# Encoder block on one core: five branch gates in the entry stage, the residual rows' work at the output projection, operands ahead of those rows in the second phase

## The chip, the cores and the metric

One Trainium2 chip, one of its cores. The metric is the device time of one execution in microseconds (us); the kernel before takes 1377.97 us as the median of three runs (1374.08 to 1382.24). A chip core has TensorE (PE, with PEld for its weight loads), VectorE (DVE), ScalarE (ACT), GpSimd (POOL) and SyncE (SP), each with an instruction stream of its own that is worked off in order; SP, ACT and POOL issue the transfers (DMA).

## The reference, cut to what matters

One encoder layer over 768 tokens of width 1024 (a prompt of 512 and a sample of 256, which are not mixed), in float32:

```python
h = layer_norm(x, ln_in_g, ln_in_b)
proj = h @ w_in + b_in                 # 512 pool | 3072 hyena | 2048 gate columns
a, u3, gl = proj[..., :512], proj[..., 512:3584], proj[..., 3584:]
ya = pool_branch(a, ...)               # four window means minus self, group linear, projection
yb = hyena_branch(u3, ...)             # short conv, two gated long FFT convolutions, projection
g = sigmoid(gl)                        # 2 x 1024 branch gates
m = g[:, :, 0] * ya + g[:, :, 1] * yb
h = layer_norm(DN_ALPHA * h + m @ w_o + b_o, ln1_g, ln1_b)
u = relu(h @ w_ff1 + b_ff1)
h = layer_norm(DN_ALPHA * h + (u * u) @ w_ff2 + b_ff2, ln2_g, ln2_b)
```

## The kernel before, in words

Every product is made of three matmuls, since each float32 operand is split into a high and a low part of a shorter format: ACT copies the raw tile to the high part (`whi`, L98), DVE computes the low part (`wlo`, L90), and PE multiplies high by high, low by high and high by low. `wsplit` (L92) does this for a weight tile that SP loads. So each weight tile costs one DMA on SP, one ACT instruction and one DVE instruction, and PE can't start on it before all three.

The program runs through these stages; the times are where they stand in the trace of before.

- Entry (0 to 45 us): layer norm of x, transposes to `hT_h`, `hT_l` (both parts of h, with the channels on the partitions). The normalised rows without scale are kept in DRAM as `d_h`.
- Entry stage (45 to 375 us): 24 jobs, each one 128-channel tile of the hyena columns (48 matmuls of 128x384 into the PSUM tiles `pa` and `pb`, short convolution, transposes `pta`, `ptb`). Between them run eight `filter_unit`s, which build the long filters' spectra: `pg` matmuls, then DVE and ACT work, a norm (`pn`), the parts `pmh` (ACT) and `pml` (DVE), and the `pk` matmuls. A list `order` with `k_after` sets after which job a filter unit starts; its second half comes after the next job.
- Before the units (375 to 400 us): three `gate_tile`s (16 tiles of 128 gate columns in all; 48 matmuls into a `pp` tile, Sigmoid on ACT, the result to DRAM as `d_s`) and the split of the transform matrix `cu` (L545 to L550).
- Units (400 to 641 us): eight hyena `unit`s, each a chain of transforms (`pf`, `p`, `pi` matmuls, with combining work on DVE between them); between units stand further gate tiles, as many as the tuple in L680 says, and four `pool_in` tiles, which also write `pp`.
- Pool windows (641 to 691 us): the window sums `pw` on DVE, group linear `pq`, the loads and splits of the hyena result `zT_h`, `zT_l`.
- hyena_out and pool_out (691 to 791 us): eight pairs, 48 `pb` and 24 `pa` matmuls each; after each of the first six a `residual_job` (L782 to L797) loads a row tile of `d_h` by POOL, multiplies it by alpha*ln_in_g, adds alpha*ln_in_b + b_o, and writes it back.
- Output projection (791 to 865 us): two groups of three row tiles by eight k steps; the `hr` rows are read from `d_h` and added (L828).
- Second phase (865 us to the end): the MLP in a scheme of seven products per block (`S forms` and the first `EARLY` products ahead, then `up_pair`s, then the down phase with products 0 to 6 and the residual rows `res` loaded by the class `Late`, L1159 to L1169).

The instruction order of each engine is not that of the Python text alone: tiles rotate through a few buffers, and a planner puts each engine's instructions in an order by their dependences. So gate matmuls fall into the chains of the units wherever these leave PE free.

Of the kernel before, what the change touches and what calls it, by code (L numbers as in the profile page):

```python
# [10 lines left out]
F32 = mybir.dt.float32  # L11
# [32 lines left out]
H = T // 2  # L44
EARLY = 7
PLAIN = 7
# [3 lines left out]
def hybrid_encoder(ctx, tc, ins, y_a, y_b):  # L50
# [387 lines left out]
    with ExitStack() as pr_stack:  # L438
# [66 lines left out]
        def x1_job(j):  # L505
            folded_tile(j, d_x1, j)

        order = [(v_job, j) for j in range(8)]
        for c in range(4):
# [3 lines left out]
        for i, (job, j) in enumerate(order):  # L513
            job(j)
            for it in pending:
                for _ in it:
                    pass
            pending = []
            if i in k_after:
                n = k_after[i]  # L520
                it = filter_unit(n % 2, n // 2)
                next(it)
                pending.append(it)
    ew_stack.close()
    k_stack.close()
# [4 lines left out]
    with ExitStack() as t_stack:  # L530
# [8 lines left out]

        gates = list(range(16))  # L540
        for _ in range(3):
            gate_tile(gates.pop(0))
# [135 lines left out]
        for n in range(8):  # L678
            unit(n // 2, n % 2)
            for _ in range((1, 1, 2, 1, 2, 0, 1, 2)[n]):  # L680
                gate_tile(gates.pop(0))
# [76 lines left out]
    def hyena_out(j):  # L758
        w = wsplit(ins["w_hy"][j])
        pb = pst("pp", "pb")  # L760
        proj(pb, w, 8, zT_h, zT_l)
        s = zl.tile([P, T], F32, tag="gt1", name="gt1", bufs=2)
        nc.sync.dma_start(s, d_s[8 + j])
        dve.tensor_tensor(by_halves(s), by_halves(pb), by_halves(s), op=ALU.mult)
        return s

    def pool_out(j, g1t):
        w = wsplit(ins["w_pp"][j], 512)
        pa = pst("pk", "pa")
        proj(pa, w, 4, ph_h, ph_l)  # L770
        s = zl.tile([P, T], F32, tag="gt0", name="gt0", bufs=2)
        nc.sync.dma_start(s, d_s[j])
        dve.tensor_tensor(by_halves(s), by_halves(pa), by_halves(s), op=ALU.mult)
        dve.tensor_tensor(s, s, g1t, op=ALU.add)
        act.copy(mT_h[:, j, :], s)
        lo_of(mT_l[:, j, :], s, mT_h[:, j, :])

    wp_stack.close()
    rj = r_stack.enter_context(pool_of("rj", 1, "right"))
    rows = {}  # L780

    def residual_job(tt):  # L782

        if not rows:
            ag, ab = (row_bc(rj, n) for n in ("ln_in_g", "ln_in_b"))
            bo = rj.tile([P, D], F32, tag="rr", name="bo_bc", bufs=2)
            nc.sync.dma_start(bo, ins["b_o"].partition_broadcast(P))
            act.activation(ag, ag, AF.Copy, scale=ALPHA)
            act.activation(ab, ab, AF.Copy, scale=ALPHA)
            dve.tensor_tensor(ab, ab, bo, op=ALU.add)  # L790
            rows["r"] = (ag, ab)
        ag, ab = rows["r"]
        t = rj.tile([P, D], F32, tag="rr", name="hres", bufs=2)
        pool.dma_start(t, d_h[tt])
        dve.tensor_tensor(t, t, ag, op=ALU.mult)
        dve.tensor_tensor(t, t, ab, op=ALU.add)
        pool.dma_start(d_h[tt], t)  # L797

    prev = hyena_out(0)
    for j in range(8):  # L800
        nxt = hyena_out(j + 1) if j < 7 else None
        pool_out(j, prev)
        prev = nxt
        if j < 6:
            residual_job(j)
    r_stack.close()
# [15 lines left out]
    raw1 = ep.tile([P, 8, H], F32, name="raw1")  # L822
    g1, b1 = (row_bc(ep, n) for n in ("ln1_g", "ln1_b"))

    def add_acc(dst, accs, halves=(0, 1)):
# [26 lines left out]
    for gr in range(2):  # L852
        accs = [[pst("acc", f"ac{t}{c}") for c in range(2)] for t in range(3)]
        hrs = []
        for t in range(3):
            hr = ep.tile([P, D], F32, tag="hr1", name="hr1", bufs=3)
            nc.sync.dma_start(hr, d_h[gr * 3 + t])
            hrs.append(hr)
        for k in range(8):
# [150 lines left out]

    ahead = {1: 7, 3: 8, 4: 9, 6: 10, 7: 11, 9: 12, 10: 13, 12: 14, 13: 15}
    first_us, first_ws = [], []
# [91 lines left out]
    def down_chunk(units, started=None):  # L1104
# [14 lines left out]

        def product(i, wsrc, out, dst, op, first):  # L1120
            us, ws = [], []
            for g in units:
                us.append(u_form(g, i))
                ws.append(split2(wsrc(g), 512, "w"))
            for t in range(3):
                o = out[t] if out else pst("y", "y")
                mult(o, us, ws, t, first)
                evacuate(dst[0], t, dst[1], o, op)

        add, sub = ALU.add, ALU.subtract  # L1130
        if started:
            for t in range(3):
                evacuate(0, t, 0, x[t])
        else:
            product(0, lambda g: b[g](0, 0), x, (0, 0), add, True)
        product(1, lambda g: b[g](1, 0), None, (0, 0), add, True)
        product(3, lambda g: grow(g, b[g](0, 0), b[g](0, 1)), z, (1, 1), add, True)
        product(4, lambda g: grow(g, run[g], b[g](1, 1)), x, (0, 1), sub, False)
# [20 lines left out]
    class Late:  # L1159


        def __init__(self):
            self.t = None

        def __getitem__(self, key):
            if self.t is None:
                self.t = rs_.tile([P, 6, D], F32, name="res")
                for tt in range(6):
                    nc.sync.dma_start(self.t[:, tt, :], d_h[tt])  # L1169
            return self.t[key]  # L1170
# [143 lines left out]
```

## Time and profile before

| | kernel before |
|---|---|
| median of three runs | 1377.97 us (1374.08 to 1382.24) |
| profiled execution | 1377.59 us, span 1375.8 us |
| PE busy | 1292.1 us, 94% of the span |
| DVE busy | 1053.1 us, 77% |
| ACT busy | 636.1 us, 46% |
| POOL busy | 92.2 us, 7% |
| mean granted clock of PE | 0.98 |
| HBM read and written | 162.79 and 68.03 MB, 168 GB/s |

The profiled execution lies 0.4 us under the median. The span is measured from the first to the last instruction; 1.8 us of the execution lie around it. Of the span PE was idle for 83.7 us (1375.8 less 1292.1), of which about 16 lie before the first matmul and 10 after the last. The granted clock is the share of its full rate that TensorE was given; it has two levels, 2.4 GHz (1.00) and 1.2 GHz (0.50), so a window's mean between them tells how much of it was spent at the lower one.

### The profile page before, as it was taken

How to read it: one execution, taken by the hardware profiler on the slowest of the kernel's cores; microseconds unless marked ns; L12 is line 12 of the kernel's file. 1: busy time of each engine (PE TensorE's matmuls, PEld its weight loads, DVE VectorE, ACT ScalarE, POOL GpSimd, SP SyncE). 2: the span in 40 equal slices, each digit the busy share in tenths (PEclk: the TensorE clock that was granted, in tenths of full speed). 3: DMA queues.
4: the chain of work that ended last, by engine and by line, in shares of the span. 5: the costliest groups of instructions: out<-in, count | busy, mean ns of one | idle time of the engine just before them, and what ended most of it. 6: DMA issues, size and time to landing. Idle time of an engine off the chain costs nothing. (4 is left out here: it accounts for less than half of the span.)

```text
span 1375.8 us, 19326 instructions
## 1 busy us (share of the span) xinstructions
PE 1292.1 (94%) x7314; PEld 1190.1 (87%) x7314; DVE 1053.1 (77%) x1625; ACT 636.1 (46%) x1026; POOL 92.2 (7%) x166
## 2 busy tenths in 40 slices
PE   5989999799989999999998999989999997999997
PEld 3879988799989999999998977879999986888885
DVE  7788888789547786878865447988877847997778
ACT  6967767566442232223421234545555643444340
POOL 1000000000000110102010000001211100000000
PEclk9999999899999999999999999999999999999999
DMA  7223442342373544434666365477756559854312
GB/s 284 85 88 119 127 138 91 113 134 101 124 273 100 189 138 162 161 120 158 198 203 214 113 228 199 140 250 283 274 186 210 190 183 313 302 179 133 93 59 92
DMA packets 94998, 232.08 MB, mean 169 GB/s; under 512 B 9936, under 2 KB 34072, under 8 KB 94905
## 3 DMA queue, kind: packets, MB, share of 16 engines
q1 hardware_dynamic: 59504, 162.50, 35.6%
q0 software_dynamic: 12896, 45.62, 8.9%
q10 hardware_dynamic: 22504, 22.73, 5.0%
q8 instruction: 57, 0.93, 0.3%
q14 instruction: 37, 0.30, 0.1%
HBM read 162.79 MB, written 68.03 MB: 168 GB/s over the span
## 5 line engine op out<-in xcount | busy, mean ns | idle before, releaser
L90 DVE TENSOR_TENSOR wlo<-raw,whi 128x1024 fp32r<-128x1024 f32 (+1 forms) x94 | 110.2, 1172 | 60.0 <-ACT whi L98 42.7
L98 ACT CAST whi<-raw 128x1024 fp32r<-128x1024 f32 (+1 forms) x76 | 76.2, 1007 | 140.5 <-PE pp L122 46.3
L1075 ACT CAST uhi<-ur 128x768 fp32r<-128x768 f32 x51 | 42.5, 835 | 111.6 <-PE x L1048 44.0
L1048 PE MATMUL x<-wlo,uhi 128*128 128x512 f32 x180 | 70.4, 392 | 0.0
L1049 PE MATMUL x<-whi,ulo 128*128 128x512 f32 x180 | 69.9, 389 | 0.0
L1047 PE MATMUL x<-whi,uhi 128*128 128x512 f32 x180 | 69.6, 389 | 0.0
L90 DVE TENSOR_TENSOR ulo<-ur,uhi 128x768 fp32r<-128x768 f32 x51 | 48.6, 953 | 15.9 <-ACT uhi L1075 15.8
L111 PE MATMUL pa<-hT_h,whi 128*128 128x384 f32 x176 | 60.3, 343 | 0.5 <-ACT whi L98 0.5
L111 PE MATMUL pa<-hT_h,wlo 128*128 128x384 f32 x176 | 60.5, 344 | 0.0
L111 PE MATMUL pa<-hT_l,whi 128*128 128x384 f32 x176 | 60.2, 342 | 0.0
L111 PE MATMUL pb<-hT_h,wlo 128*128 128x384 f32 x176 | 60.0, 341 | 0.0
L111 PE MATMUL pb<-hT_l,whi 128*128 128x384 f32 x176 | 59.9, 341 | 0.0
L111 PE MATMUL pb<-hT_h,whi 128*128 128x384 f32 x176 | 59.9, 340 | 0.0
L111 PE MATMUL pk<-pmh,ck_h 128*128 128x256 f32 x160 | 45.8, 303 | 13.4 <-ACT pmh L393 13.4
L569 ACT CAST vh<-t 128x512 fp32r<-128x512 f32 x24 | 14.9, 621 | 88.5 <-DVE t L568 88.5
L121 PE MATMUL pp<-hT_h,whi 128*128 128x384 f32 x160 | 54.0, 338 | 0.0
L122 PE MATMUL pp<-hT_l,whi 128*128 128x384 f32 x160 | 54.0, 338 | 0.0
L120 PE MATMUL pp<-hT_l,whi 128*128 128x384 f32 x160 | 54.0, 337 | 0.0
L123 PE MATMUL pp<-hT_h,wlo 128*128 128x384 f32 x160 | 53.9, 337 | 0.0
L124 PE MATMUL pp<-hT_h,wlo 128*128 128x384 f32 x160 | 53.8, 336 | 0.0
L119 PE MATMUL pp<-hT_h,whi 128*128 128x384 f32 x160 | 53.8, 336 | 0.0
L111 PE MATMUL pk<-pml,ck_h 128*128 128x256 f32 x160 | 47.8, 303 | 1.8 <-DVE pml L90 1.8
(341 smaller groups left out, 4440.6 us busy)
## 6 DMA issues: line engine op xcount, KB each, us to landing
raw<-in_w_in SPq DMA_DIRECT2D x44, 512.0 KB, 3.7
ur<-d_u SPq DMA_DIRECT2D x51, 384.0 KB, 3.1
raw<-in_w_ff SPq DMA_DIRECT2D x32, 512.0 KB, 3.9
w<-in_w_ff SPq DMA_DIRECT2D x64, 256.0 KB, 5.3
d_k<-ko POOLq DMA_DIRECT2D x24, 512.0 KB, 3.1
kt<-d_k SPq DMA_DIRECT2D x24, 512.0 KB, 3.5
d_u<-us POOLq DMA_DIRECT2D x56, 192.0 KB, 4.3
d_u<-u ACTq DMA_DIRECT2D x50, 192.0 KB, 3.3
```

The lines of the kernel that those rows point to most:

```text
L90: (eng or dve).tensor_tensor(dst, src, hi.bitcast(F32), op=ALU.subtract)
L98: act.copy(hi[:, :n], raw[:, :n])
L111: pe.matmul(out, l, r, start=(n == 0), stop=(n == len(seq) - 1))
L119: pe.matmul(a, wh[:, ws], xh[:, k, :H], start=first, stop=False)
L120: pe.matmul(a, wh[:, ws], xl[:, k, :H], start=False, stop=False)
L121: pe.matmul(b, wh[:, ws], xh[:, k, H:T], start=first, stop=False)
L122: pe.matmul(b, wh[:, ws], xl[:, k, H:T], start=False, stop=False)
L123: pe.matmul(a, wl[:, ws], xh[:, k, :H], start=False, stop=last)
L124: pe.matmul(b, wl[:, ws], xh[:, k, H:T], start=False, stop=last)
L1047: pe.matmul(out, a, h, start=first and j == 0, stop=False, skip_group_check=not first)
L1048: pe.matmul(out, a, m, start=False, stop=False, skip_group_check=not first)
L1049: pe.matmul(out, l, h, start=False, stop=j == n - 1, skip_group_check=not first)
```

## The change

Four edits stand in one diff.

1. Five of the sixteen branch gates (columns 0 to 4 of the pool branch's gate) are computed in the entry stage by a new `early_gate`, after the first half of a filter unit, in `pa` and `pb`. They are stored before the sigmoid (ACT Identity), and `pool_out` applies the Sigmoid in place after loading such a gate. Ahead of the units stand four gate tiles instead of three, and the tuple of gate tiles between the units falls from (1, 1, 2, 1, 2, 0, 1, 2) to (1, 1, 1, 0, 1, 0, 0, 1), so that two remain behind them instead of three.
2. `residual_job` is gone. The rows alpha*ln_in_g and alpha*ln_in_b + b_o are loaded at the output projection (three broadcasts of 512 KB by SP), and each `hr` row tile gets its multiplication and addition there.
3. `EARLY` is 8 instead of 7, and the table `ahead` follows.
4. At the start of the down phase the operands of products 1 and 3 are loaded and split before the started product's sums are evacuated, and `Late` loads a half row when it is first asked for, instead of six whole row tiles at the first access.

```diff
-EARLY = 7
+EARLY = 8
...
+        def early_gate(j):
+
+            w = wsplit(ins["w_in"][G_T + j])
+            ps = (pst("pa", "pa"), pst("pb", "pb"))
+            st = sg.tile([P, T], F32, tag="st", name="st")
+            for dst, sl in zip(ps, (slice(0, H), slice(H, T))):
+                acc(dst[:, :H], [(w[0][:, k * P : (k + 1) * P], w[1][:, k * P : (k + 1) * P], hT_h[:, k, sl], hT_l[:, k, sl])
+                                 for k in range(8)])
+                act.activation(st[:, sl], dst[:, :H], AF.Identity, bias=col("b_in", G_T + j), scale=1.0)
+            act.dma_start(d_s[j], st)
+            plain_gates.add(j)
...
                 pending.append(it)
+                if i in (2, 6, 8, 10, 12):
+                    early_gate(gates.pop(0))
...
-        for _ in range(3):
+        for _ in range(4):
             gate_tile(gates.pop(0))
...
-            for _ in range((1, 1, 2, 1, 2, 0, 1, 2)[n]):
+            for _ in range((1, 1, 1, 0, 1, 0, 0, 1)[n]):
                 gate_tile(gates.pop(0))
...
         nc.sync.dma_start(s, d_s[j])
+        if j in plain_gates:
+            act.activation(s, s, AF.Sigmoid)
         dve.tensor_tensor(by_halves(s), by_halves(pa), by_halves(s), op=ALU.mult)
...
-        t = rj.tile([P, D], F32, tag="rr", name="hres", bufs=2)
-        pool.dma_start(t, d_h[tt])
-        dve.tensor_tensor(t, t, ag, op=ALU.mult)
-        dve.tensor_tensor(t, t, ab, op=ALU.add)
-        pool.dma_start(d_h[tt], t)
...
+    for dst, name in ((ar[:, 0], "ln_in_g"), (ar[:, 1], "ln_in_b"), (bo, "b_o")):
+        nc.sync.dma_start(dst, ins[name].partition_broadcast(P))
+    act.activation(ar[:, 0], ar[:, 0], AF.Copy, scale=ALPHA)
+    dve.scalar_tensor_tensor(ar[:, 1], ar[:, 1], ALPHA, bo, op0=ALU.mult, op1=ALU.add)
...
             nc.sync.dma_start(hr, d_h[gr * 3 + t])
+            dve.tensor_tensor(hr, hr, ar[:, 0], op=ALU.mult)
+            dve.tensor_tensor(hr, hr, ar[:, 1], op=ALU.add)
...
-    ahead = {1: 7, 3: 8, 4: 9, 6: 10, 7: 11, 9: 12, 10: 13, 12: 14, 13: 15}
+    ahead = {1: 8, 3: 9, 5: 10, 6: 11, 8: 12, 10: 13, 11: 14, 13: 15}
...
         if started:
+            one = operands(1, lambda g: b[g](1, 0))
+            three = operands(3, t1)
             for t in range(3):
                 evacuate(0, t, 0, x[t])
+            multiply(one, None, (0, 0), add, True)
+            multiply(three, z, (1, 1), add, True)
...
-                for tt in range(6):
-                    nc.sync.dma_start(self.t[:, tt, :], d_h[tt])
+            tt, cs = key[1], key[2]
+            for c in range(2):
+                if (tt, c) not in self.got and cs.start in (None, c * 512):
+                    self.got.add((tt, c))
+                    sl = slice(c * 512, (c + 1) * 512)
+                    nc.sync.dma_start(self.t[:, tt, sl], d_h[tt][:, sl])
```

On PE in the entry stage, the matmuls between the norm `pn` of the first filter unit and the first `pk` matmul of its spectrum were none; before:

```order
287 L111 MATMUL pb<-hT_h,whi 128x384
288 L111 MATMUL pb<-hT_l,whi 128x384
289 L422 MATMUL pn<-ident,nr 128x1 x2
290 L111 MATMUL pk<-pmh,ck_h 128x256 x2
291 L485 MATMUL pta<-ident,ft 128x128 x4
292 L489 MATMUL ptb<-ident,ft 128x128 x2
293 L111 MATMUL pa<-hT_h,wlo 128x384
```

and after the change, where 18 matmuls of a gate (`pa`, then `pb`) stand between the two:

```order
291 L111 MATMUL pa<-hT_l,whi 128x384
292 L422 MATMUL pn<-ident,nr 128x1 x2
293 L111 MATMUL pa<-hT_h,wlo 128x384
294 L111 MATMUL pa<-hT_h,whi 128x384
295 L111 MATMUL pa<-hT_l,whi 128x384
296 L111 MATMUL pa<-hT_h,wlo 128x384
297 L111 MATMUL pa<-hT_h,whi 128x384
```

For the second unit's first spectrum it is the other way round. Before, 15 `pa` matmuls followed its `pn`:

```order
475 L111 MATMUL pa<-hT_h,wlo 128x384
476 L422 MATMUL pn<-ident,nr 128x1 x2
477 L111 MATMUL pa<-hT_h,whi 128x384
478 L111 MATMUL pa<-hT_l,whi 128x384
479 L111 MATMUL pa<-hT_h,wlo 128x384
480 L111 MATMUL pa<-hT_h,whi 128x384
```

and after the change its `pk` follows at once:

```order
472 L111 MATMUL pb<-hT_l,whi 128x384
473 L422 MATMUL pn<-ident,nr 128x1 x2
474 L111 MATMUL pk<-pmh,ck_h 128x256 x2
475 L485 MATMUL pta<-ident,ft 128x128 x4
476 L489 MATMUL ptb<-ident,ft 128x128 x2
477 L111 MATMUL pk<-pml,ck_h 128x256
```

On PE at the end of the units, the last `p` matmul of the eighth unit was followed by 97 gate matmuls (`pp`); before:

```order
3692 L111 MATMUL p_6301<-cu_h,vh 128x128
3693 L111 MATMUL p_6301<-cu_l,vh 128x128
3694 L111 MATMUL p_6301<-cu_h,vl 128x128
3695 L124 MATMUL pp<-hT_h,wlo 128x384
3696 L119 MATMUL pp<-hT_h,whi 128x384
3697 L120 MATMUL pp<-hT_l,whi 128x384
3698 L121 MATMUL pp<-hT_h,whi 128x384
```

and after the change by the group linear of the pool branch (`pq`); the `pp` matmuls all stand earlier:

```order
3890 L111 MATMUL p_6427<-cu_h,vh 128x128
3891 L111 MATMUL p_6427<-cu_l,vh 128x128
3892 L111 MATMUL p_6427<-cu_h,vl 128x128
3893 L111 MATMUL pq<-qh,wph 128x512
3894 L111 MATMUL pq<-ql,wph 128x512
3895 L111 MATMUL pq<-qh,wpl 128x512
3896 L111 MATMUL pq<-qh,wph 128x256
```

From the last `pi` matmul of the seventh unit to that point there were 111 `pp` matmuls, and there are 16 now; behind it, up to the first `pa` matmul, there were 193 `pp`, 24 `pq` and 64 `pb`, and there are 24 `pq` and 115 `pb`.

On SP at the start of the down phase, the six residual row tiles (`res`) stood behind the operands of product 1 (`ur` and `w`) and ahead of those of product 3; before:

```order
218 L1081 DMA ur<-d_u 128x768
219 L1097 DMA w_11007<-in_w_ff 128x512 x2
220 L1081 DMA ur<-d_u 128x768
221 L1097 DMA w_11008<-in_w_ff 128x512 x2
222 L1169 DMA res<-d_h 128x1024 x6
223 L1081 DMA ur<-d_u 128x768
224 L1097 DMA w_11007<-in_w_ff 128x512 x4
225 L1081 DMA ur<-d_u 128x768
226 L1097 DMA w_11008<-in_w_ff 128x512 x4
```

and after the change the half rows stand behind both:

```order
209 L1088 DMA ur<-d_u 128x768
210 L1104 DMA w_10998<-in_w_ff 128x512 x2
211 L1088 DMA ur<-d_u 128x768
212 L1104 DMA w_10999<-in_w_ff 128x512 x2
213 L1088 DMA ur<-d_u 128x768
214 L1104 DMA w_10998<-in_w_ff 128x512 x4
215 L1088 DMA ur<-d_u 128x768
216 L1104 DMA w_10999<-in_w_ff 128x512 x4
217 L1192 DMA res<-d_h 128x512 x6
```

## Rows read from the trace of the kernel before

**Rows 1.** The head of the page: the span, and the line of TensorE (PE) with busy us, share of the span and number of instructions.

```profile
span 1375.8 us, 19326 instructions
...
PE 1292.1 (94%) x7314; PEld 1190.1 (87%) x7314; DVE 1053.1 (77%) x1625; ACT 636.1 (46%) x1026; POOL 92.2 (7%) x166
```

**Rows 2.** The waits of PE over the whole span; columns: what waited and for what, us in total, times, longest us.

```profile
PE pk L111 <- ACT pmh L393: 13.4, 8, 2.8
PE pb L123 <- DVE wlo L90: 7.8, 2, 5.5
PE z L1047 <- ACT whi L1075: 7.3, 1, 7.3
PE pi L111 <- ACT vh L569: 5.4, 1, 5.4
PE z L912 <- ACT whi L922: 2.8, 1, 2.8
```

**Rows 3.** PE and the others in four stretches of 25 us; columns: from:to, length, busy us with (xcount) of PE, PEld, DVE, ACT, POOL, then the granted clock of PE, the DMA share and GB/s.

```profile
75.00:100.00 25.00, 22.06 (x125) 20.21 (x126) 20.84 (x48) 14.68 (x30) 1.06 (x2) 0.86 0.39 122
250.00:275.00 25.00, 22.26 (x127) 20.31 (x127) 17.84 (x40) 15.29 (x34) 1.07 (x2) 0.88 0.39 121
400.00:425.00 25.00, 19.65 (x132) 19.33 (x132) 14.74 (x18) 6.62 (x11) 0.00 (x0) 0.86 0.54 188
725.00:750.00 25.00, 19.50 (x99) 19.19 (x98) 14.04 (x15) 3.68 (x5) 2.67 (x5) 0.86 0.63 213
```

**Rows 4.** The same view and columns by stage: the entry stage, the last two units' end (from the last `pi` matmul of unit 6 to the last `p` matmul of unit 7), from there to the first `pa` matmul of the pool branch, and the start of the second phase.

```profile
45.00:375.00 330.00, 311.44 (x1910) 290.47 (x1910) 271.73 (x530) 218.48 (x431) 17.39 (x32) 0.96 0.36 117
601.80:641.10 39.30, 39.21 (x269) 37.56 (x268) 31.34 (x42) 12.55 (x22) 3.61 (x4) 1.00 0.24 81
641.10:691.40 50.30, 49.13 (x281) 47.85 (x281) 44.85 (x52) 23.16 (x36) 5.35 (x6) 1.00 0.61 208
1126.90:1146.00 19.10, 9.62 (x39) 6.47 (x37) 10.49 (x13) 5.21 (x6) 0.00 (x0) 0.94 1.00 376
```

**Rows 5.** The same view of the instructions of one tile alone: the first two rows are of `pp` (columns PE, PEld, ACT), the third of `pb` (PE, PEld, DVE, ACT), the fourth of `pq` (PE, PEld, DVE).

```profile
601.80:641.10 39.30, 21.35 (x112) 18.89 (x112) 2.39 (x6) 1.00 0.24 81
641.10:691.40 50.30, 34.02 (x193) 33.16 (x192) 5.09 (x9) 1.00 0.61 208
...
641.10:691.40 50.30, 11.62 (x64) 11.11 (x65) 0.96 (x1) 0.00 (x0) 1.00 0.61 208
...
641.10:691.40 50.30, 5.62 (x24) 4.16 (x24) 4.30 (x4) 1.00 0.61 208
```

**Rows 6.** The timeline of PE; columns: start, us, engine and line, operation, out<-in, then in brackets the idle time before it and what ended it. The first two are the first and the 91st matmul of one unbroken row of gate matmuls, the third is the first `pk` matmul of a filter spectrum in the entry stage.

```profile
641.13 0.34 PE L119 MATMUL pp<-hT_h,whi 128*128 128x384 f32 x1
...
656.73 0.33 PE L119 MATMUL pp<-hT_h,whi 128*128 128x384 f32 x1
...
245.53 0.50 PE L111 MATMUL pk<-pmh,ck_h 128*128 128x256 f32 x2 [2.75 <-ACT pmh L393]
```

**Rows 7.** The timeline around 405 us, of ACT, of DVE and of PE (one of the last `pf` matmuls ahead of a wait).

```profile
404.76 0.62 ACT L549 CAST cu_h<-craw 128x512 fp32r<-128x512 f32 x1 [1.48 <-DMA craw<-in_cu]
...
408.53 1.22 DVE L566 TENSOR_TENSOR t<-pf,kt 128x1024 f32<-128x1024 f32 x1
...
402.93 0.28 PE L111 MATMUL pf<-abh,cu_l 128*128 128x256 f32 x1
```

**Rows 8.** The timeline of DVE at the end of the units: two low halves of gate weights that are computed there.

```profile
605.47 1.22 DVE L90 TENSOR_TENSOR wlo<-raw,whi 128x1024 fp32r<-128x1024 f32 x1
...
622.90 1.22 DVE L90 TENSOR_TENSOR wlo<-raw,whi 128x1024 fp32r<-128x1024 f32 x1
```

**Rows 9.** The timeline of DVE, and of POOL, in the stage of hyena_out and pool_out.

```profile
732.28 1.23 DVE L795 TENSOR_TENSOR hres<-hres,bc_ln_in_g 128x1024 f32<-128x1024 f32 x1 [5.16 <-DMA hres<-d_h]
733.42 0.95 DVE L764 TENSOR_TENSOR gt<-pb,gt 128x768 f32<-128x768 f32 x1
734.29 1.21 DVE L90 TENSOR_TENSOR wlo<-raw,whi 128x1024 fp32r<-128x1024 f32 x1
...
726.61 0.53 POOL L794 DMA_DIRECT2D hres<-d_h  x1 [5.16 <-DMA d_h<-hres]
```

**Rows 10.** The timeline of SP's DMA issues at the start of the output projection, and two lines of DVE in the same stage.

```profile
798.35 1.42 SPq L857 DMA_DIRECT2D hr<-d_h  x3
802.81 36.59 SPq L95 DMA_DIRECT2D raw<-in_w_o  x8
...
814.57 1.22 DVE L90 TENSOR_TENSOR wlo<-raw,whi 128x1024 fp32r<-128x1024 f32 x1 [1.71 <-ACT whi L98]
817.56 1.23 DVE L90 TENSOR_TENSOR wlo<-raw,whi 128x1024 fp32r<-128x1024 f32 x1 [1.76 <-ACT whi L98]
```

**Rows 11.** The chain that ended last around 1130 us (start, us, what), and SP's issues there.

```profile
1128.62 8.20 DMA res<-d_h
1136.84 7.22 DMA ur<-d_u
...
1127.31 4.00 SPq L1169 DMA_DIRECT2D res<-d_h  x6
1131.35 0.71 SPq L1081 DMA_DIRECT2D ur<-d_u  x1
...
1136.84 0.33 SPq L1081 DMA_DIRECT2D ur<-d_u  x1
```

More of the change, by code (lines that the diff above doesn't have):

```diff
@@ L506, in x1_job @@
             folded_tile(j, d_x1, j)
+        gates = list(range(16))
+        plain_gates = set()
+        def early_gate(j):
[8 more added lines that the diff above has]
+            plain_gates.add(j)
         order = [(v_job, j) for j in range(8)]
@@ L538, in gate_tile @@
             act.dma_start(d_s[j], st)
-        gates = list(range(16))
-        for _ in range(3):
+        for _ in range(4):
             gate_tile(gates.pop(0))
@@ L763, in hyena_out @@
         nc.sync.dma_start(s, d_s[8 + j])
+        if 8 + j in plain_gates:
+            act.activation(s, s, AF.Sigmoid)
         dve.tensor_tensor(by_halves(s), by_halves(pb), by_halves(s), op=ALU.mult)
@@ L772, in pool_out @@
         nc.sync.dma_start(s, d_s[j])
+        if j in plain_gates:
+            act.activation(s, s, AF.Sigmoid)
         dve.tensor_tensor(by_halves(s), by_halves(pa), by_halves(s), op=ALU.mult)
@@ L778, in hybrid_encoder @@
     wp_stack.close()
[L779 to L792, printed above, removed]
-        t = rj.tile([P, D], F32, tag="rr", name="hres", bufs=2)
-        pool.dma_start(t, d_h[tt])
-        dve.tensor_tensor(t, t, ag, op=ALU.mult)
-        dve.tensor_tensor(t, t, ab, op=ALU.add)
-        pool.dma_start(d_h[tt], t)
     prev = hyena_out(0)
@@ L803, in hybrid_encoder @@
         prev = nxt
-        if j < 6:
-            residual_job(j)
     r_stack.close()
@@ L823, in hybrid_encoder @@
     g1, b1 = (row_bc(ep, n) for n in ("ln1_g", "ln1_b"))
+    ar = ep.tile([P, 4, 4, P], F32, tag="sm", name="ar", bufs=1).rearrange("p (r a) b c -> p r (a b c)", r=2)
+    bo = ep.tile([P, D], F32, tag="hr1", name="bo", bufs=3)
+    for dst, name in ((ar[:, 0], "ln_in_g"), (ar[:, 1], "ln_in_b"), (bo, "b_o")):
+        nc.sync.dma_start(dst, ins[name].partition_broadcast(P))
+    act.activation(ar[:, 0], ar[:, 0], AF.Copy, scale=ALPHA)
+    dve.scalar_tensor_tensor(ar[:, 1], ar[:, 1], ALPHA, bo, op0=ALU.mult, op1=ALU.add)
     def add_acc(dst, accs, halves=(0, 1)):
@@ L1118, in grow3, with operands @@
             return b[g](0, 1)
-        def product(i, wsrc, out, dst, op, first):
+        def operands(i, wsrc):
             us, ws = [], []
@@ L1124, in product, with multiply @@
                 ws.append(split2(wsrc(g), 512, "w"))
+            return us, ws
+        def multiply(ops, out, dst, op, first):
             for t in range(3):
                 o = out[t] if out else pst("y", "y")
-                mult(o, us, ws, t, first)
+                mult(o, *ops, t, first)
                 evacuate(dst[0], t, dst[1], o, op)
+        def product(i, wsrc, *rest):
+            multiply(operands(i, wsrc), *rest)
         add, sub = ALU.add, ALU.subtract
+        t1 = lambda g: grow(g, b[g](0, 0), b[g](0, 1))
         if started:
+            one = operands(1, lambda g: b[g](1, 0))
+            three = operands(3, t1)
             for t in range(3):
                 evacuate(0, t, 0, x[t])
+            multiply(one, None, (0, 0), add, True)
+            multiply(three, z, (1, 1), add, True)
         else:
             product(0, lambda g: b[g](0, 0), x, (0, 0), add, True)
-        product(1, lambda g: b[g](1, 0), None, (0, 0), add, True)
-        product(3, lambda g: grow(g, b[g](0, 0), b[g](0, 1)), z, (1, 1), add, True)
+            product(1, lambda g: b[g](1, 0), None, (0, 0), add, True)
+            product(3, t1, z, (1, 1), add, True)
         product(4, lambda g: grow(g, run[g], b[g](1, 1)), x, (0, 1), sub, False)
@@ L1163, in __init__ @@
             self.t = None
+            self.got = set()
         def __getitem__(self, key):
```

## The prediction

> **What bounds the kernel now.** I read the head of the page first: PE is busy for 1292.1 of 1375.8 us [rows 1], so the time is PE's work plus what PE loses. Second the waits of PE [rows 2], which name the losses: 13.4 us in eight waits of `pk` on ACT's `pmh`, 7.8 us of `pb` on `wlo`, 7.3 us of `z` on a weight's high part, 5.4 us of `pi`, 2.8 us of another `z`. Third the windows, for the granted clock, since after a wait PE may run at half rate: 0.86 around 75 and 400 us and around 725 us, 0.88 at 250 us [rows 3]. A window of 25 us at 0.86 has lost 25 x 0.14 = 3.5 us. Over the entry stage the mean is 0.96, 330 x 0.04 = 13 us lost, beside 330 - 311.4 = 18.6 us of idle time [rows 4]. So the whole that can be had is small, and it has to be read stage by stage; and in two places PE is not waiting only because gate matmuls stand there.
>
> **The five gates in the entry stage.** A gate has 48 matmuls. One unbroken row of gate matmuls takes (656.73 - 641.13) / 90 = 0.173 us apiece [rows 6], so a gate is 8.3 us of PE and five are 41.6 us, which come here and go elsewhere. What counts is PE's idle time. The matmuls now stand in the waits between a norm and the spectrum behind it. The row of such a wait shows 2.75 us [rows 6], and 18 matmuls between the two are 3.1 us: that wait is gone. Others keep theirs: the waits ahead of the first gate can't change, and the second unit's first spectrum loses its 15 matmuls of cover, which gives a new wait of about the same 2.75 us. Of 18.6 us I count half, 9.4, as saved (6 to 13), and of the 13 us of clock half, 6.6, with the waits that cause it. Each gate adds a weight split and a store, but DVE is busy 271.7 of 330 us here and ACT 218.5 [rows 4]; five weight splits of 1.2 us [rows 8], and about as much on ACT, hide there. Gain 16 (10 to 20).
>
> **The fourth gate ahead of the units.** The wait of `pi`, 5.4 us [rows 2], comes about so: `pf` was done at about 403, DVE took up its combination (L566) only at 408.53, since the splits of `cu` stand before it in DVE's order and ACT's half of them waited for transfers (404.76) [rows 7]. With 48 more matmuls, 8.3 us, ahead of the first `pf`, that list is through. The 5.4 us go, and with them the low clock that follows, 3.5 us in the window from 400 us [rows 3]. Gain 8.8 (5 to 9).
>
> **The end of the units.** Here the gates are missed. From the last `pi` of unit 6 to the last `p` of unit 7 PE was busy 39.2 of 39.3 us, with 111 `pp` matmuls (the view counts 112, one cut by its edge) [rows 4, 5]. Now 16 are left: 39.2 - 95 x 0.173 = 22.8 us of work. The chain through DVE stays. It can't have been longer than 39.3; two weight splits of 1.2 us leave it [rows 8], and PE's part in it may run at the lower clock after waits, some 3 us the other way. I take 38 us, so 15 us of new idle time (11 to 19). From the last `p` to the first `pa` PE had 193 `pp`, 34 us, and waited hardly (49.1 of 50.3) [rows 4, 5]. Now the work is 24 `pq`, 5.6 us [rows 5], and 115 `pb` at 0.173, 19.9: 25.5 us. DVE decides. It had 52 instructions and 44.9 us here [rows 4]; by the order it has 49 now, 49 x 44.85 / 52 = 42.3 us, and some 2 us of waits for ACT and PE in its list, 44 in all. Idle time of PE: 44 - 25.5 = 19 us (15 to 26). Loss together 34.
>
> The Trainium skill has a rule for this (Perfetto Trace Analysis, Optimization Strategy): where a kernel's most-contended engine changes over time, interleave the regimes. It speaks against this move, since gate matmuls stood beside the DVE work and now stand in the PE-bound stage. The trace agrees in that PE was 98% busy there although DVE was 89% busy (44.85 of 50.3); by it alone, without the entry's waits, the move would be a loss of 34 us, and by the rows it is 34 less 24.8.
>
> **The residual rows.** In the order of DVE the row work waits for POOL's load: 5.16 us at 732.28, and the weight's low part behind it (734.29) is what PE waits for [rows 9]; POOL had the load after the write-back ahead of it (726.61). The 7.8 us of `pb` waits [rows 2] and the 3.5 us of low clock at 725 us [rows 3] go. The five sigmoids come in, but ACT is busy 3.7 of 25 us there [rows 3]. Gain 11 (8 to 11.5). At the output projection SP now issues three broadcasts behind the layer norm's two and ahead of the `hr` rows, and all stand ahead of the weight that was issued at 802.81 [rows 10]. DVE gets seven instructions of 1.2 us, the size of L795 [rows 9], in one block between the weight splits that ran at 814.57 and 817.56 [rows 10], where 1.7 us were idle: 8.5 less 1.7 is 6.8 us, and the weights are split ahead of PE's need by a lead that no row shows by itself; with 5 us for it, 2 us of wait are left. None at all if the loads come early, 8 if the whole block shows. Loss 2 (0 to 8).
>
> **One more early product.** The `z` wait of 2.8 us [rows 2] has 24 more matmuls, 4.2 us, ahead of it; the weight it waits for is pushed back too. Gain 2 (0 to 4).
>
> **The start of the down phase.** In 1126.9 to 1146 PE worked 9.6 of 19.1 us while the transfers were full, share 1.00 and 376 GB/s [rows 4]. The chain shows why: `res` took 8.20 us from 1128.62, and `ur` of product 3 landed 7.22 us later [rows 11]. With `res` behind them, the operands come ahead. The Trainium skill says (DMA: Bandwidth & Descriptors, Queues, rings and completion order) that on each transfer engine descriptors are consumed in ring order, and SP has one row of rings; `ur` landing just one `res` later agrees. By that rule the whole 8.2 us could be won. By the rows the bytes are the same, and the six rows are needed for the first evacuations, where `y` now waits for them: I take 5 us, of 9.5 idle (2 to 8).
>
> **The sum,** made against the profiled 1377.6: -16 - 8.8 + 34 - 11 + 2 - 2 - 5 = -6.8. I give 3 back for PE's share of the stretch after the units at the lower clock (windows after a wait show 0.86, so 3.5 us in 25 [rows 3]): -3.8, 1373.8. The median of the runs is 0.4 higher, so 1374.
>
> **Rivals.** *A, clearly faster.* The tail costs less: without the gate matmuls in between, each step of the units' chain starts sooner, and both idle terms come at their low ends, 11 + 15 = 26 instead of 34, while the entry stage gives 20 instead of 16. That is 12 us: 1362. For it speaks that PE never waited in that stretch, so its chain's true length is not seen; against it that DVE was busy 31.3 of 39.3 us [rows 4].
>
> *B, slower: DVE sets the pace from the last `pi` to the first `pa`, and PE falls to half rate.* PE then has long waits and 22.8 + 25.5 = 48 us of work, of which the parts between DVE's steps can't be hidden. If 14 us of it double (11 beyond the 3 counted) and the idle time stands at 19 + 22 instead of 34, it is 1374 + 11 + 7 = 1392. It decides from about 45 us lost in this stretch. For it speak the 0.86 windows after waits of only 5 us; against it that the `pb` matmuls there are free to stand in the waits.
>
> *C, the change doesn't do what it says in the entry stage.* ACT's `pmh` and DVE's `pml` come later by what the gates add there, and the waits stay: the 16 us fall away, 1390. Against it: 58 us of DVE are idle in that stage [rows 4].
>
> **How the numbers follow.** Forecast 0.50, A 0.29, B 0.14, C 0.07. About 0.5%, 6.9 us, is what a measurement of this kernel can tell from no change: under 1371.1 is faster, over 1384.9 slower. The forecast's own range is 1366 to 1383, of which 0.10 lies under 1371. So faster 0.10 + 0.29 = 0.39, same 0.39, slower 0.14 + 0.07 and 0.01 of the forecast = 0.22. The range takes half of A and most of B and C: 1359 to 1391.
>
> **What would show it.** The waits of `pk` on `pmh` fall from 13.4 to about 7; the wait of `pi` on `vh` is gone from 400 us; PE shows waits of some 15 us together in the last unit and some 19 up to the first `pa`, with clocks under 1.00 there; the `pb` waits on `wlo` around 700 to 735 are gone; a wait of 1 to 3 us on `wlo` at about the seventh weight of `w_o`; the start of the down phase keeps 4 to 5 us of idle time. It is wrong if the stretch between the last `pi` of unit 6 and the first `pa` is not near 38 + 44 = 82 us (89.6 before), or if the entry stage grows by much else than 41.6 - 16 = 26 us.

## The result and the profile after

The changed kernel takes 1393.45 us (median of four runs, 1390.72 to 1395.29), beside 1376.38 us for the one before in the same comparison: a ratio of 1.0115, 95% interval 1.0084 to 1.0147. It is 1.15% slower, some 16 us, outside the stated range of 1359 to 1391. The profiled execution took 1392.77 us with a span of 1391.0 us, 15.2 us more than that of before. A difference in us that stands behind a ratio below is that ratio times the time of the kernel before. The profiled execution of before (1377.59 us) lies 3.5 us above the median of its 25 runs beside the first experiments (1374.14), so that the stage differences of the first four kernels below add up to 2 to 6 us less than their ratios say.

The head of the page of the changed kernel, and its granted clock in 40 slices of 34.8 us (tenths of full rate), against [rows 1]:

```profile
span 1391.0 us, 19323 instructions
...
PE 1298.9 (93%) x7314; PEld 1193.3 (86%) x7314; DVE 1054.5 (76%) x1625; ACT 639.4 (46%) x1035; POOL 85.7 (6%) x154
...
PEclk9999999999999999998599999999999999999999
```

PE has the same number of matmuls and 6.8 us more busy time, since it ran some at the lower rate: the two slices with 8 and 5, from 626 to 696 us, hold the end of the units. The waits of PE in the changed kernel (who waited for whom, us in total, times, longest us), against [rows 2]:

```profile
PE pq L111 <- ACT qh L744: 11.8, 1, 11.8
PE p L111 <- ACT vh L585: 5.0, 2, 3.9
PE pt L852 <- DVE ln_mv L137: 4.7, 1, 4.7
PE pf L111 <- ACT abh L585: 4.2, 2, 2.9
...
PE pk L111 <- ACT pmh L393: 3.5, 2, 1.9
PE ac L841 <- ACT whi L98: 2.6, 1, 2.6
```

All the waits that the prediction wanted gone are gone or smaller: `pk` on `pmh` fell from 13.4 to 3.5 us, and `pi` on `vh`, `pb` on `wlo` (7.8 to 1.0) and `z` of the second phase (7.3 to 1.6) are no longer at the top. New ones stand in their place: `pq`, `p` and `pf` at the end of the units, `pt` and `ac` in the output projection. By stage, from the same view of windows as [rows 4], for the last two units, from there to the first `pa`, and for the output projection; the changed kernel:

```profile
627.70:671.90 44.20, 31.24 (x174) 28.77 (x173) 30.27 (x41) 8.19 (x14) 3.56 (x4) 0.74 0.19 60
671.90:719.90 48.00, 31.36 (x138) 28.04 (x138) 40.22 (x49) 19.45 (x32) 5.31 (x6) 0.74 0.46 151
800.50:883.60 83.10, 72.30 (x314) 57.67 (x313) 61.02 (x85) 27.58 (x35) 1.64 (x3) 0.96 0.56 200
```

and the kernel before, the two stretches that [rows 4] doesn't have:

```profile
641.10:697.10 56.00, 54.83 (x314) 53.55 (x314) 44.85 (x52) 24.22 (x37) 5.92 (x7) 1.00 0.65 215
791.50:865.80 74.30, 69.55 (x315) 56.15 (x313) 46.49 (x72) 26.23 (x34) 1.60 (x3) 1.00 0.56 203
```

The reader should compare PE's busy time with the length, and the clock behind POOL's column: 31.2 of 44.2 us at 0.74, then 31.4 of 48.0 at 0.74, where PE had been busy nearly throughout at 1.00. A name in [rows 4] has to be set right here: the stretch there that ends at 691.4 us ends with the last low part of the pool branch on DVE (`ph_l`), not with the first `pa` matmul. That one started at 697.1, with 96 `pb` ahead of it since the last `p`, not 64; in the changed kernel 111 started ahead of it, not 115. So 15 `pb` came forward from the pairs. The table uses 697.1.

Stage lengths in us, from the starts of the first or last matmul of a kind in PE's timeline. The predicted change is that of the prediction's terms, with the matmuls that moved (41.6 us of gates into the entry, 48 `pp` more, 8.3, up to the last `pi` of unit 6, 288 `pp` of 0.173 us, 49.9, out of the units' end, 15 `pb`, 2.6, forward from the pairs):

| stage | before | changed | predicted change | measured change |
|---|---|---|---|---|
| start to the first `pp` | 374.9 | 399.4 | +25.6 | +24.5 |
| to the last `pi` of unit 6 | 226.7 | 228.3 | -0.5 | +1.6 |
| to the first `pa` of the pairs | 95.5 | 92.2 | -10.3 | -3.3 |
| the pairs, to the first `ac` | 94.4 | 80.6 | -13.6 | -13.8 |
| the output projection, to the first `y` | 74.2 | 83.1 | +2 | +8.9 |
| to the first product of the down phase | 261.9 | 265.7 | -2 | +3.8 |
| to the end | 248.1 | 241.7 | -5 | -6.4 |
| all | 1375.8 | 1391.0 | -3.8 | +15.2 |

Four of seven terms are within 2.1 us. Three are off by 6 to 7 us each, all the same way: the units' end, the output projection, and the stretch of the early products. Stages that no edit touches differ between the profiled kernels too, by some 3 us, so the last of the three is the least certain.

### The profile page after: what moved, and what is told of

Same layout as the page of the kernel before. It is cut to its first block, busy times and chain, and to the rows that moved or that the text cites. A ratio compares the mean times of both kernels' runs of the same rounds, so it can differ in the third digit from the quotient of the medians.

```text
span 1391.0 us, 19323 instructions
## 1 busy us (share of the span) xinstructions
PE 1298.9 (93%) x7314; PEld 1193.3 (86%) x7314; DVE 1054.5 (76%) x1625; ACT 639.4 (46%) x1035; POOL 85.7 (6%) x154
## 5 line engine op out<-in xcount | busy, mean ns | idle before, releaser
L1082 ACT CAST uhi<-ur 128x768 fp32r<-128x768 f32 x51 | 42.6, 835 | 101.1 <-PE x L1055 37.3
L111 PE MATMUL pa<-hT_h,whi 128*128 128x384 f32 x216 | 73.8, 342 | 0.0
L111 PE MATMUL pa<-hT_h,wlo 128*128 128x384 f32 x216 | 73.6, 341 | 0.0
L111 PE MATMUL pb<-hT_h,whi 128*128 128x384 f32 x216 | 73.1, 338 | 0.0
L111 PE MATMUL pb<-hT_l,whi 128*128 128x384 f32 x216 | 73.0, 338 | 0.0
L90 DVE TENSOR_TENSOR ulo<-ur,uhi 128x768 fp32r<-128x768 f32 x51 | 48.7, 955 | 14.2 <-ACT uhi L1082 14.1
L111 PE MATMUL pf<-abh,cu_h 128*128 128x256 f32 x160 | 46.4, 295 | 4.8 <-ACT abh L585 4.2
L929 ACT CAST whi<-t 128x1024 fp32r<-128x1024 f32 x32 | 33.5, 1046 | 36.4 <-PE x L920 33.2
L919 PE MATMUL y<-a_h,whi 128*128 128x384 f32 x128 | 44.1, 345 | 5.2 <-ACT sp L941 3.6
L111 PE MATMUL pf<-abl,cu_h 128*128 128x256 f32 x160 | 46.6, 293 | 1.3 <-DVE abl L90 1.1
L919 PE MATMUL z<-s_h,whi 128*128 128x384 f32 x128 | 43.5, 340 | 3.8 <-ACT whi L929 2.2
L111 PE MATMUL pf<-abh,cu_l 128*128 128x256 f32 x160 | 46.2, 290 | 0.0
```

The lines of the kernel that those rows point to most:

```text
L90: (eng or dve).tensor_tensor(dst, src, hi.bitcast(F32), op=ALU.subtract)
L111: pe.matmul(out, l, r, start=(n == 0), stop=(n == len(seq) - 1))
L919: pe.matmul(out, wh, xh, start=first and k == 0, stop=False, skip_group_check=not first)
L929: act.copy(hi[:, :n], src)
L1082: act.copy(hi, src)
```

## The experiments

### Each edit alone

The first four kernels are the kernel before with one of the four edits of the diff each: the gates (`early_gate`, the four gate tiles, the tuple, the Sigmoid later); the residual rows; `EARLY` and `ahead`; the operands ahead of the rows, with `Late` in half rows.

> The first edit alone: five gates in the entry stage, four ahead of the units, five between them, two behind. By the stages of the changed kernel's trace against the one before, the entry grows by 24.0 us, the stretch before the units by 9.1, from the first pf to the last pi of unit 6 it falls by 7.4, from there to the first pa it grows by 2.9, and the pairs behind it fall by 8.8 (51 pb matmuls already done): +19.8, so about 1396 us. Theory 1 (this edit carries the whole loss, because PE runs at half clock through the units' end): 1392 to 1399, with the granted clock of the stretch from the last pi of unit 6 to the first pa well under 0.8. Rival (the prediction's own sum, -16 - 8.8 + 34 + 3 = +12): 1388, with that stretch at 82 us.

Measured: 1385.9 us, 1.0095 (1.0065 to 1.0125), +13 us. The size is below theory 1 and near the rival, but for other reasons than the rival gave: the stretch from the last `pi` to the first `pa` took 90.8 us at a clock of 0.75 and 0.80, near what theory 1 has, not 82. What theory 1 missed lies behind it: the eight pairs fell from 94.4 to 83.0 us with the residual rows still in them, and the 15 `pb` that came forward are only 2.6 of that. (The expectation counted 51 `pb`, from the 64 set right above.) The pairs before, with the first edit alone, and in the changed kernel, one line each:

```profile
697.10:791.50 94.40, 86.46 (x481) 85.50 (x481) 52.00 (x55) 18.48 (x23) 5.88 (x11) 0.96 0.55 177
716.90:799.90 83.00, 81.07 (x466) 80.51 (x466) 51.22 (x54) 20.94 (x26) 6.45 (x12) 1.00 0.64 216
719.90:800.50 80.60, 80.60 (x466) 80.60 (x466) 36.32 (x41) 18.81 (x24) 0.00 (x0) 1.00 0.40 126
```

PE's idle time there falls from 7.9 to 1.9 us and its clock rises to 1.00 though DVE still does the row work (51.22 us busy). So 8.8 us of what the residual rows cost go away with the first edit too, and on top of it the second edit brings 2.4 more in the pairs. Why the rows no longer hold PE up there was not followed.

> The second edit alone: the residual rows' multiplication and addition at the output projection. Theory (the stages of the changed kernel's trace: 11.3 us won in the eight pairs, 8.8 lost in the output projection, where SP stands still 9 us on the third row tile ahead of the weights): -2.5, 1374 us, with the waits on the weights of w_o there. Rival (the prediction's terms, 11 won and 2 lost): -9, 1367.

Measured: 1377.44 us, 1.0031 (1.0012 to 1.0049): slightly slower, about 4 us. The pairs fell by 11.2 us and the output projection rose by 8.9, as read from the changed kernel. Both theories have the time under that of before, and it isn't; that this edit by itself is worth 9 us is excluded.

> The third edit alone: eight early products instead of seven and the table that follows. Theory (stages of the changed kernel: 2.8 us more up to the first z, 0.9 more up to the first product of the down phase): +3.7, 1380 us, with a few more waits of about 1 us among the up products. Rival (the prediction's term): -2, 1374.

Measured: 1375.86 us, 1.0014 (0.9993 to 1.0035): no difference that can be measured. In its profile the stages from the first `y` to the down phase took 2.0 us more. In the changed kernel they took 3.8 more. Over all the kernels here, those without this edit took 260.2 to 263.0 us there and those with it 263.1 to 265.7: no gain is borne out, and how much it costs is not shown.

> The fourth edit alone: the operands of products 1 and 3 ahead of the residual rows, which come in halves. Theory (from the first product of the down phase to the end the changed kernel takes 6.3 us less): -6.3, 1370 us, with no wait over 2 us at the start of the down phase. Rival (the prediction's term): -5, 1371.5; rival two, that the rows are only late elsewhere: 1376.

Measured: 1365.64 us, 0.9945 (0.9922 to 0.9967), -7.6 us. From the first product of the down phase to the end it took 241.0 us instead of 248.1. The wait of `z` there, 7.28 us before, was 1.70; in the changed kernel it was 1.64:

```profile
1158.75 0.96 PE L1054 MATMUL z<-whi,uhi 128*128 128x512 f32 x3 [1.64 <-ACT whi L1082]
```

This edit does what the prediction said, and a little more. The four alone add up to +11.6 us, together they are +15.8. With intervals of 2.5 to 4 us on each, these times alone don't show that the edits meet. The stages show one place where they do: 8.8 us in the pairs are won by the first edit and by the second, and only once by both.

### What makes the units' end long

```diff
             for _ in range((1, 1, 1, 0, 1, 0, 0, 1)[n]):
                 gate_tile(gates.pop(0))
+            for _ in range((0, 0, 0, 0, 0, 0, 1, 2)[n]):
+                pp = pst("pp", "pp")
+                proj(pp, (hT_h[:, 0, :], hT_l[:, 0, :]), 6, hT_h, hT_l)
```

> The first edit alone with 108 more matmuls of 128x384 after units 7 and 8, on operands that are there already (h by h, into pp, never read): 18.7 us more work for PE, none for DVE, ACT or the queues. Theory 1 (half of the loss at the units' end is PE's low clock in the chain between DVE's steps): the low clock goes, the stretch from the last pi of unit 6 to the first pa falls from 90.8 us (first edit alone) to 82 to 86, and the time falls from 1386 to about 1379, though there is more work. Rival (DVE alone sets the stretch, the clock costs nothing): 90.8 us still, 1386. Second rival (the matmuls land in the way of the chain): over 95 us, 1391 or more.

Measured: 1384.76 us, 1.0080 (1.0050 to 1.0110), and 89.7 us for the stretch. As a whole theory 1 fails and the rival's numbers come out: the time can't be told from that of the first edit alone. The two halves tell more. The same windows as above, first of the kernel with the first edit alone:

```profile
626.10:670.60 44.50, 31.32 (x174) 28.75 (x173) 30.24 (x41) 8.17 (x14) 3.56 (x4) 0.75 0.18 60
670.60:716.90 46.30, 29.04 (x139) 25.27 (x139) 40.01 (x49) 19.52 (x32) 5.31 (x6) 0.80 0.48 157
```

and of the one with the added matmuls:

```profile
624.00:663.90 39.90, 39.85 (x275) 38.59 (x274) 31.18 (x42) 10.08 (x16) 3.61 (x4) 1.00 0.26 83
663.90:713.70 49.80, 31.95 (x148) 28.52 (x148) 41.50 (x50) 20.65 (x33) 3.84 (x6) 0.76 0.51 164
```

Nearly all of the added matmuls ended up in the two units: PE has 101 more there (275 and 174), and 9 more behind the last `p` (148 and 139). In the units PE does 17.5 us more work, its clock stays at 1.00, and the two units take 4.6 us less: 39.9 us, nearly the 39.3 of before. DVE's busy time there is nearly the same (30.2 and 31.2). So in the units at least 4.6 us of the loss were the low clock in PE's own steps of the chain, and it is shown. Behind the last `p`, where hardly anything was added, the wait of `pq` grew from 11.8 to 14.8 us, at a clock of 0.76, and the half from 46.3 to 49.8 us: DVE was busy 1.5 us longer there (one more weight split) and idle 2.0 us longer. That ate up most of what the units won; how much the clock costs in this half by itself was not shown.

### How many gates the entry can take

```diff
-                if i in (2, 6, 8, 10, 12):
+                if i in (2, 8):
...
-            for _ in range((1, 1, 1, 0, 1, 0, 0, 1)[n]):
+            for _ in range((1, 1, 2, 1, 1, 0, 1, 2)[n]):
```

> The first edit with two early gates instead of five (behind the second and the fourth filter unit's first half), four ahead of the units and the others where they stood before; of the 304 pp matmuls behind the last pi of unit 6, 160 stay. Theory 1 (the loss comes only when PE runs dry there): no wait over 1.5 us and no low clock up to the last p, 86 us from the last pi of unit 6 to the first pa, entry stage 9 to 10 us longer than before, and the time 6 to 9 us under before: 1366. Rival (what is moved out of the units' end is lost one for one): the time of before, 1374, or 2 to 4 us over it.

Measured: 1358.68 us, 0.9896 (0.9867 to 0.9924), -14 us, twice what was expected. The entry stage shows most of why. PE in 45 to 370 us, before, with five early gates (the changed kernel) and with two, one fence each:

```profile
45.00:370.00 325.00, 306.44 (x1881) 285.47 (x1881) 270.73 (x529) 217.23 (x428) 16.07 (x30) 0.96 0.36 116
```

```profile
45.00:370.00 325.00, 318.05 (x1980) 298.24 (x1980) 266.09 (x509) 216.30 (x420) 15.53 (x29) 0.98 0.37 121
```

```profile
45.00:370.00 325.00, 318.04 (x1987) 298.75 (x1987) 274.39 (x532) 222.38 (x436) 16.20 (x31) 0.98 0.37 123
```

With two gates PE is as busy (318.04 of 325 us, at 0.98) as with five (318.05, 0.98): its idle time falls from 18.6 to 7.0 us in both. The waits of `pk`, 13.4 us before, are 3.5 us in both:

```profile
PE pk L111 <- ACT pmh L393: 3.5, 2, 1.9
```

So two gates take away every wait that five do. They stand behind two of the eight filter units, but the order of what follows changes with them: before, three of the norms `pn` had no matmul between them and the spectrum behind (at 82, 188 and 254 us), and with two gates one has none (at 112 us). The stage up to the first `pp` takes 373.2 us with 16.6 us more in it, no more than in the profiled kernels that have the entry of before (371.9 to 374.9). The other three gates cost 399.4 - 373.2 = 26.2 us there in the changed kernel, 8.7 each, and 25.1 with the first edit alone: their full price. At the units' end the 160 `pp` that are left keep PE busy to the last `p`, and the wait stands behind it alone:

```profile
602.20:641.60 39.40, 39.31 (x270) 37.55 (x268) 31.36 (x42) 12.20 (x20) 3.63 (x4) 1.00 0.27 91
641.60:691.90 50.30, 38.59 (x187) 35.09 (x187) 43.36 (x51) 20.43 (x33) 5.34 (x6) 0.87 0.53 168
```

The whole stretch is 89.7 us instead of 95.5, with a clock of 0.87 in the second half: 24.9 us of gate work (144 `pp`) left it, 2.6 of `pb` came in, and it got 5.8 us shorter. With five gates another 24.9 us are gone from it, and it takes 90.8 us (first edit alone) and 92.2 (changed kernel), no less. So the 14 us are made of an entry that takes no longer, 5.8 us at the units' end and 9.5 in the pairs, which fall from 94.4 to 84.9 us with the residual rows still in them, as with the first edit.

Then the same two gates in all four edits:

> All four edits as in the changed kernel, but two early gates instead of five and the other gates where they stood before (160 of the pp matmuls stay behind the last pi of unit 6). Theory (five gates were too many, and that alone makes the changed kernel slower than the one before): 25 to 29 us under the changed kernel, 1364 to 1368, about 8 us under before. Rival (the other edits carry part of the loss): 1372 or more.

Measured: 1366.59 us, 0.9932 (0.9912 to 0.9951), and 24.4 us under the changed kernel by the two spans. The theory holds, at the lower edge of its gain: three gates too many turn a gain of 0.7% into a loss of 1.15%. And with the fourth edit alone beside the two gates:

> The same two early gates with the fourth edit (operands ahead of the residual rows in the second phase). Theory: the two do not touch each other, so the gains add, 8 and 7.6: 1359. Rival (they share a wait): 1364 or more.

Measured: 1353.16 us, 0.9848 (0.9820 to 0.9876), -21 us, the fastest here. -14 and -7.6 add up, and the rival falls. Its span is 13.5 us under that of all four edits with two gates, so the second and third edits together still cost there: the output projection took 85.0 us with them and 74.9 without.

```diff
-                if i in (2, 8):
+                if i in (2, 8, 12):
...
-        for _ in range(4):
+        for _ in range(3):
             gate_tile(gates.pop(0))
```

> The fourth edit with three early gates (behind the second, fourth and sixth filter unit's first half), three gates ahead of the units, and the same 160 pp matmuls behind the last pi of unit 6. Theory (in the entry each gate takes waits away as long as there are any, and ahead of the units the fourth gate saves a wait of 5.7 us and its low clock): both are worth about 8 us a gate, so 1353 as with two and four, plus or minus 3. Rival (the entry's waits are used up by two): 1358.

Measured: 1362.16 us, 0.9918 (0.9889 to 0.9948), 9 us behind the kernel with two early gates and four ahead of the units, and 4 behind the rival's number. The rival's reason holds: the third gate lengthens the entry from 372.8 to 381.4 us, 8.6, its full price. Beside it, three gates ahead of the units leave the wait of `pi`, 6.8 us, as the theory has it:

```profile
PE pi L111 <- ACT vh L585: 6.8, 1, 6.8
PE pk L111 <- ACT pmh L393: 3.5, 2, 1.9
```

### What makes the output projection long

```diff
-    bo = ep.tile([P, D], F32, tag="hr1", name="bo", bufs=3)
+    bo = ep.tile([P, D], F32, name="bo")
```

> The second edit alone with a buffer of its own for the b_o broadcast, so that the third row tile's load waits for none. Theory (SP stands on that load for 9 us ahead of the weights of w_o): SP's issue of the three hr rows falls from 9.4 to about 1.5 us, the output projection falls from 83.1 us (second edit alone) to 76 to 78, and the time from 1377 to about 1371. Rival (the transfers themselves, 1.5 MB of broadcasts and 1.5 MB of rows ahead of the weights, or the 8.5 us of DVE work in one block, are the cause): 81 to 83 us, 1376.

Measured: 1376.45 us, 1.0027 (1.0008 to 1.0047). SP's issues, first with the second edit alone, then here (start, us, what):

```profile
790.29 10.50 SPq L842 DMA_DIRECT2D hr<-d_h  x3
800.88 31.81 SPq L95 DMA_DIRECT2D raw<-in_w_o  x8
```

```profile
785.11 1.89 SPq L842 DMA_DIRECT2D hr<-d_h  x3
788.21 42.72 SPq L95 DMA_DIRECT2D raw<-in_w_o  x8
```

SP is free again after 1.9 us instead of 10.5, and it helps nothing: the stage takes 86.9 us instead of 83.1. The theory falls, and with it my reading that a wait of SP is the cause. Why the stage takes 3.8 us more was not followed.

```diff
-    for dst, name in ((ar[:, 0], "ln_in_g"), (ar[:, 1], "ln_in_b"), (bo, "b_o")):
-        nc.sync.dma_start(dst, ins[name].partition_broadcast(P))
...
-            dve.tensor_tensor(hr, hr, ar[:, 0], op=ALU.mult)
-            dve.tensor_tensor(hr, hr, ar[:, 1], op=ALU.add)
+            dve.tensor_tensor(hr, hr, g1, op=ALU.mult)
+            dve.tensor_tensor(hr, hr, b1, op=ALU.add)
```

> The second edit alone without the three broadcasts and their combination (the rows are multiplied by ln1_g and added to ln1_b, which are there already, in place of alpha*ln_in_g and alpha*ln_in_b + b_o). 1.5 MB less stand ahead of the weights of w_o; the six DVE instructions per group stay, and so does PE's order (24 matmuls of the second group ahead of the first transpose, where before had 42). Theory (the bytes make the weights late): the first group takes 34 to 35 us instead of 37.3 (second edit alone) and the stage 79 to 80 instead of 83.1. Rival (the DVE block): 82 to 83.

Measured, in a single execution (the first group is taken from the start of the first to that of the 144th `ac` matmul): first group 34.4 us, stage 80.2, 1369.81 us. The theory holds: without the broadcasts the first group is 2.9 us shorter (37.3 with the second edit alone), close to the 33.8 of the kernel before.

```diff
-            dve.tensor_tensor(hr, hr, ar[:, 0], op=ALU.mult)
-            dve.tensor_tensor(hr, hr, ar[:, 1], op=ALU.add)
```

> The second edit alone without the twelve DVE instructions on the rows (the rows are added unscaled); the broadcasts and the loads stay, and PE's order too. Theory (the bytes make the weights late): the first group still 36 to 37 us, the stage 82 to 83. Rival (the DVE block of 8 us between two weight splits): first group 34, stage 79 to 80. In both theories the wait of the first transpose stays at 4 to 5 us, since 18 matmuls of the second group no longer stand ahead of it.

Measured, in a single execution: first group 36.4 us, stage 82.3, 1374.02 us. The block of DVE work that the prediction counted is worth 0.9 us, no more than the first group differs by among the kernels with the second edit as it stands (37.2 to 38.3); the bytes ahead of the weights are worth 2.9. In both, the wait of the first transposes stays, 4.7 us. It was 1.25 before, and is 4.67 in the changed kernel:

```profile
836.56 1.06 PE L847 MATMUL pt<-ident,hr 128*128 128x128 f32 x8 [1.25 <-DVE ln_mv L137]
848.24 1.30 PE L852 MATMUL pt<-ident,hr 128*128 128x128 f32 x5 [4.67 <-DVE ln_mv L137]
```

Before, 42 matmuls of the second group stood between the first group's end and these transposes; in every kernel with the second edit it is 24, 18 less, 18 x 0.23 = 4.1 us less cover. Why the program's order comes out so is not settled: it does so without the broadcasts and without the row work as well. So of the 8.9 us, 3 go to the bytes and at most 1 to DVE. At the transposes PE waits 3.4 us more (4.67 after 1.25), and over the stage it is busy 72.3 us instead of 69.5 for the same matmuls, at a clock of 0.96 instead of 1.00: these two are most of the rest, and that the missing cover causes them follows from the order, not from a run that puts it back.

## Why the prediction was wrong

It was wrong in sign and range: it forecast 1374, no change, and 1393 was measured.

**Sized right.** The entry's gain of 16 came out as 41.6 - 24.5 = 17.1 (idle time 11.6 less, where 9.4 was counted). The residual rows' 11 came out as 13.8 - 2.6 = 11.2 in the pairs. That this fits is partly luck, since 8.8 of it come with the first edit already. The down phase's 5 came out as 6.4 in the changed kernel and 7.6 alone. The wait of `pi` went, with 6.7 (8.3 less 1.6) for the 8.8.

**The units' end, 34 + 3.** The prediction named its own test here, a stretch near 38 + 44 = 82 us: 48.3 of work (22.8 and 25.5) and 34 of idle time. It took 44.2 + 48.0 = 92.2: PE was busy 31.2 + 31.4 = 62.6 us and idle 13.0 + 16.6 = 29.6. So the idle time was counted well, 4 us too high, and the step that failed is the price of the lower clock. The prediction has it twice: "some 3 us the other way" ahead of the 38, and "I give 3 back for PE's share of the stretch after the units at the lower clock". The matmuls, four `pb` fewer than counted, took 14 us longer than the 48.3. The prediction priced the low clock from windows with one wait of 5 us, 0.86; here PE waits again and again, and two windows of 44 and 48 us stand at 0.74. Most of the miss lies in the last two units, 44.2 us for the 38, and at least 4.6 of those 6.2 us are shown to be the clock, by the filled kernel. Behind them it took 48.0 us for 44 + 3, but not as counted: DVE was busy 40.2 us, where 42.3 were counted, and idle 7.8 instead of the "some 2 us of waits for ACT and PE"; what the clock costs there is not shown. Rival B had the mechanism of the clock: it put 14 us on it, as measured, but 41 on the idle time, where 29.6 were. Its 1392 is near the measured time only because the next two terms came on top.

The Trainium skill says that interleaving the regimes may improve a kernel whose most-contended engine changes over time (Perfetto Trace Analysis, Optimization Strategy). The traces agree as far as the gate work finds waits: with two gates in the entry and 160 `pp` left at the units' end, PE is busy 318.0 of 325 us in the one and 39.3 of 39.4 in the last two units, though only 38.6 of 50.3 behind them.

**The output projection, 2 (0 to 8).** It cost 8.9. The step that failed is the one that starts at "DVE gets seven instructions of 1.2 us", as the only cost of the stage: that block is worth at most 0.9. The three broadcasts ahead of the weights, which the prediction saw but gave no time of their own, are worth 2.9, and most of the rest lies at a later place, the transposes, where 18 matmuls of cover fell away; the prediction had not looked at the order there.

**One more early product, -2.** It came out as +3.8 in the stage of the changed kernel and as nothing measurable alone. The 24 matmuls do shorten the wait of that `z` (2.8 to 2.2), but PE's waits in the whole stretch grow from 11.6 to 14.2 us. How much of the 3.8 is the edit's stays open: the kernel with two early gates and all four edits took 263.1 us there, and the one with the first and the fourth alone 263.0.

What the prediction didn't ask at all is the one that matters most: how much of the entry's gain each gate brings. It took five gates as one term, 16 for 41.6, and the net of the move as given. Two bring all of it; the other three bring nothing, neither in the entry nor at the units' end. That is the loss: with two gates instead of five the four edits are 0.7% faster than before.

## What to carry to other kernels

When filler work is moved into waits, price it piece by piece: here the first two pieces filled the waits, each further one cost its whole length, and where those came from they had cost nothing. Where filler is taken out of a chain between two engines, price the lower clock of TensorE beside the idle time: here its matmuls took 14 us longer beside 30 us of idle time, and at least 4.6 of the 14 lengthened the chain. And price transfers that are put ahead of a stage's weights: here 1.5 MB cost 2.9 us, and setting the issuing engine free won nothing.

## What had not been expected of the hardware

Useless matmuls made a stretch shorter: 17.5 us of them in the last two units took it from 44.5 to 39.9 us, with the granted clock at 1.00 instead of 0.75. The whole kernel was no faster for it (1384.76 and 1385.9 us), since the stretch behind got longer.
